# Relative bias table of a two-layer encoder: one copy in DRAM, read back with a positive step on SyncE's queue

## The chip, the cores and the metric

The kernel runs on one core of one Trainium2 chip. A time is the device time of one execution in microseconds (us); the kernel before takes 1199.93 us, the median of three runs (1199.75 to 1200.17). Engines are named as in the profile: PE is TensorE, DVE is VectorE, ACT is ScalarE, POOL is GpSimd, SP is SyncE. SP computes nothing here and only issues DMAs, which it does in the order of its program; SPq and ACTq in a row are the instructions by which SP and ACT issue DMAs.

## The reference

Two layers of an encoder over 256 tokens of width 1024, all float32:

```python
for i in range(DEPTH):                                       # DEPTH = 2
    h = x + 0.5 * swiglu(rms_norm(x, norm_ffn1[i]), w_ffn1_in[i], w_ffn1_out[i])   # D_FF = 2816
    u = rms_norm(h, norm_mix[i])
    q, k, v, c, g = split(u @ w_in[i])
    q, k = rms_norm per head (q_norm, k_norm)                # 8 query heads, 2 key heads of 64
    y_attn = window_attention(q, k, v, sink[i], rel_bias) @ w_attn_out[i]
    y_conv = silu(layer_norm(depthwise_conv(...))) @ w_conv_out[i]
    h = h + (sigmoid(g_attn) * y_attn + sigmoid(g_conv) * y_conv) @ w_o[i]
    h = h + 0.5 * swiglu(rms_norm(h, norm_ffn2[i]), w_ffn2_in[i], w_ffn2_out[i])
    x = h + (p[i] @ w_pe_proj[i]) * sigmoid(rms_norm(h, norm_pe[i]) @ w_pe_gate[i])
```

What the change is about lies in `window_attention`. The scores of a query at place q (0 to 127) of its block against a window of 384 keys get a bias that depends on the distance alone:

```python
rel = kj[None, :] - BLOCK - qi[:, None]          # qi: 0..127, kj: 0..383
bias = rel_bias[t5_buckets(rel)]                 # one value for each distance and head
s = where(valid, s + bias, NEG_INF)              # valid: |rel| <= 128 and inside the sequence
```

So the bias of one head is a table of 512 distances, and row q of the 128 x 384 matrix is that table shifted by one place for each q. The table and the matrix are the same in both layers.

## The kernel before

**Activations** lie with features on partitions, as blocks of 128 features by 256 tokens. Matrix products are made exact to float32 by splitting both operands into two float32r parts (hi and lo) and adding three products: lines 311, 312 and 313 in `mm3`.

**The weight stream** (class `Weights`) sets the pace of the work. SP loads raw weights in units of up to 1,024 KB into four buffers (line 76). From each unit, ACT casts a piece of 128 columns to its hi part (line 100) and DVE subtracts to get the lo part (line 101); such a piece is a spec. With every spec that PE takes (`get`), ACT and DVE are told to prepare the spec six further on (`LOOK`), and SP to load the unit two beyond its unit. Seven specs (`W_BUFS`) have room for their two parts. A raw buffer is free again when the casts and subtractions of its unit are done; then SP may issue the load of the unit four further on, and not before, and whatever DMA stands behind that load in SP's program waits with it.

**A feed-forward stage** (`ffn`) has 22 steps `gate_up(j)`, each two specs of 24 matmuls into one PSUM tile `ps_gu`, and then 8 steps `down(f)` into `ps_fo`. The evacuation of a step runs on DVE and ACT while PE does the next step. `hooks` is a table from j to a function that is called ahead of step j. In the first feed-forward stage of layer 0 it builds what later stages need: `late_loads` ahead of step 1 (small parameter loads, on SP's queue), `late_params` ahead of step 5, and `late_tables` ahead of step 6.

**The bias** is made in `late_tables`: a one-hot matrix of 33 x 512 picks the table of 8 heads x 512 distances with one product (`ps_rb`, line 522), DVE copies it to `tb` on 8 partitions (line 524), and then ACT issues two DMAs. The first (line 526) writes the table 128 times, once for each query, to the DRAM tile `tb_d` (128 x 8 x 512). The second (line 530) reads it back into `bias`, 128 partitions x 8 heads x 384, with a step that is one element short of a copy's length from partition to partition, so that partition q starts at place 127 - q. It reads what the first has written, so ACT waits for the first to land before it issues the second.

**The order** of the instructions on each engine comes from a scheduler that plays the program through with costs; it may move an instruction ahead of others by its priority. DMAs that are marked `keep_in_program_order` stay where the program puts them.

**The attention** runs inside the mixer (`mix`). `queries` transposes the normed queries into PSUM (`ps_qt`), and ACT copies them to `qT` (line 730), heads by tokens. `scores` multiplies a block of 128 queries with the keys (`ps_s`, line 745), so that queries lie on the partitions, and DVE adds the slice of `bias` (line 755). `gather` makes the output for the block (`ps_o`, line 792), with the queries along the free axis, and ACT copies it to `o` (line 799), which the products with `w_attn_out` (`ps_ao`, line 837) read later.

Of the kernel before, what the change touches and what calls it, by code (L numbers as in the profile page):

```python
# [15 lines left out]
P = 128  # L16
# [25 lines left out]
class Weights:  # L42
    """Streams the weights: DMA of raw float32 blocks, and their exact split into two
    float32r parts, in the order in which the tensor engine takes them. A spec without
    parts hands the raw block itself to the tensor engine."""

# [12 lines left out]
    def spec(self, k, n, pieces):  # L59
        """pieces: (unit, first k of the unit, first column of the unit, first column here, columns)."""  # L60
        self.specs.append((k, n, pieces, False))
# [53 lines left out]
    def later(self, n, fn):  # L115
        """Runs fn in front of the n-th get from here."""
        self.hooks.append((self.next_get + n - 1, fn))
# [21 lines left out]
def encoder_kernel(ctx: ExitStack, tc: tile.TileContext, a: dict, out: bass.AP):  # L139
# [17 lines left out]

    # ---------------------------------------------------------------- inputs
    ident = const.tile([P, P], F32, name="ident")
# [36 lines left out]

    # --------------------------------------------------------- weight stream
    ws = Weights(tc, raw_pool, w_pool)
# [90 lines left out]

    # ------------------------------------------------------------- constants  # L290
    ones_d = const.tile([P, P], F32, name="ones_d")
# [11 lines left out]

    # -------------------------------------------------------------- helpers
    def mm3(ps, w, x, first=True, last=True, k0=0, x_k0=0, n_k=None, cols=slice(0, P)):
# [9 lines left out]
    def pair(name, x, fresh):  # L315
        """Two products with x in one PSUM tile [P, 2, T]; right behind the evacuation that
        made x (fresh) its last block comes last."""
        if not fresh:
            ps = mm_tile(name).rearrange("p (c t) -> p c t", c=2)
            return ps, [lambda c=c: mm3(ps[:, c, :], ws.get(), x) for c in range(2)]  # L320
        ps = at_tile(name).rearrange("p (c t) -> p c t", c=2)[:, :, :T]
        w = []

        def start(c):
            w.append(ws.get())
            mm3(ps[:, c, :], w[c], x, last=False, n_k=KD - 1)

        def end():
            start(1)
            for c in range(2):  # L330
                mm3(ps[:, c, :], w[c], x, first=False, k0=KD - 1, x_k0=KD - 1, n_k=1)

        return ps, [lambda: start(0), end]
# [15 lines left out]
    def flush_urgent():  # L349
        """The last evacuation of a phase, which the next one waits for."""  # L350
        with tc.high_priority(offset=300):
            flush()

    def group(products, evac):
        """The products of one PSUM bank; its evacuation follows the first product of the next group."""
        for i, fn in enumerate(products):
            fn()
            if i == 0:
                flush()
        pending.append(evac)  # L360
# [8 lines left out]
    def newton(r, v, n):  # L369
        """r <- r * (1.5 - 0.5 * v * r * r)"""  # L370
        t = tmp.tile([P, n], F32, name="nwt", tag=f"nwt{n}")
        nc.gpsimd.tensor_tensor(out=t, in0=r, in1=r, op=ALU.mult)
        nc.gpsimd.tensor_tensor(out=t, in0=t, in1=v, op=ALU.mult)
        nc.gpsimd.tensor_scalar(out=t, in0=t, scalar1=-0.5, scalar2=1.5, op0=ALU.mult, op1=ALU.add)
        nc.gpsimd.tensor_tensor(out=r, in0=r, in1=t, op=ALU.mult)

    def table(func):
        """Loads a table of the scalar engine ahead of its use."""
        tc.keep_in_program_order(nc.scalar.preload_act_table(func))

    class gate:
        """Evacuations wait for the norm of the phase that they belong to."""

        ready = True

    class Stat:
        """The reciprocal root mean square r of x over its features, on every partition;
        with tokens on partitions as r_tok, and what it makes of eps behind it as eps_tok."""

# [39 lines left out]
    def emit_x(k, gain, xn, stat):  # L429
        """The next layer's operand x * gain of feature block k, split, and its squares."""  # L430
        src = x32[:, k, :]
        nc.scalar.activation(out=xn[0][:, k, :], in_=src, func=AF.Copy, scale=gain)
        nc.vector.scalar_tensor_tensor(
            out=xn[1][:, k, :], in0=src, scalar=gain, in1=xn[0][:, k, :].bitcast(F32),
            op0=ALU.mult, op1=ALU.subtract,
        )
        stat.add(src)
# [8 lines left out]

    # -------------------------------------------------------------- startup
    x_cur = new_x("xa", "x0")
# [28 lines left out]

    # tables for later phases, built while the first phase runs
    late = {}
# [25 lines left out]
    def late_tables(hp):  # L505
# [18 lines left out]
        nc.vector.tensor_copy(tb, ps[:NH, :NREL])  # L524
        tb_d = dram.tile([P, NH, NREL], F32, name="tb_d")
        nc.scalar.dma_start(tb_d.rearrange("q h m -> h q m"), tb.unsqueeze(1).broadcast_to([NH, P, NREL]))
        bias = const.tile([P, NH, 3 * P], F32, name="bias")
        base = tb_d[:, :, :]
        skew = bass.AP(base.tensor, base.offset + P - 1, [[NH * NREL - 1, P], [NREL, NH], [1, 3 * P]])
        nc.scalar.dma_start(bias, skew)  # L530
        late["bias"] = bias

    # ------------------------------------------------------------------ FFN
    def ffn(hp, l, x_in, stat_in, gain_name, xn, stat, hooks):
# [45 lines left out]

    # ---------------------------------------------------------------- mixer
    def mix(l, u, st, xn, stat):
        cw, kg, bias, sink = (late[n] for n in ("cw", "kg", "bias", "sink"))
        with tc.tile_pool(name="mix_pool", bufs=1) as mp:
# [18 lines left out]

            # ------------------------------------------------ gated conv input
            def conv_in(i):
# [20 lines left out]

            # ------------------------------------------- keys and values by token
            vt = mp.tile([P, 2, P], F32, name="vt")
# [3 lines left out]
            def head_norms(ps, heads):  # L632
                """1 / rms of each head, by token; eps stands behind the norm of x that ps has not seen."""
                n = 2 * heads
# [58 lines left out]

            # ------------------------------------------------- queries by token
            qn = mp.tile([P, 2, GROUP, 2, HD], F32, name="qn", tag="sqq")
            qT = mp.tile([P, GROUP, T], F32, name="qT")

            def queries():
# [23 lines left out]
                def turn():  # L722
                    pt = at_tile("ps_qt").rearrange("p (c t) -> p c t", c=GROUP)
                    for c in range(GROUP):
                        for t in range(2):
                            nc.tensor.transpose(
                                pt[:, c, t * P : (t + 1) * P], qn[:, t, c].rearrange("p v d -> p (v d)"), ident
                            )
                    for c in range(0, GROUP, 2):
                        nc.scalar.copy(out=qT[:, c : c + 2, :], in_=pt[:, c : c + 2, :])  # L730

# [3 lines left out]

            # -------------------------------------------------------- attention
            o = mp.tile([P, GROUP, T], F32, name="o")
# [49 lines left out]
            def gather(qb, v):  # L787
# [9 lines left out]
                if v == 1:  # L797
                    ov = o_ps.pop(qb).rearrange("p (c q) -> p c q", c=GROUP)
                    nc.scalar.copy(out=o[:, :, qb * P : (qb + 1) * P], in_=ov)

            # ------------------------------------------------------------ gates
            for at, fn in (
# [28 lines left out]

            # ----------------------------------------------------- branch outputs
            def products(ps, x):
# [75 lines left out]
            def mix_out(f, n):  # L909
                """Blocks f .. f + n; behind conv_out the first blocks take its last part at the end."""  # L910
                ps = at_tile("ps_wo").rearrange("p (c t) -> p c t", c=2)[:, :, :T] if n == 2 else None
# [31 lines left out]

    # --------------------------------------------------- per-layer embedding
    def embed(l, x_in, st, xn, stat):
# [64 lines left out]
    for l in range(L):  # L1010
        with tc.tile_pool(name="ffn1_pool", bufs=1) as hp:
            hooks = {1: lambda: late_loads(hp), 5: late_params, 6: lambda: late_tables(hp)} if l == 0 else {}
            xn, stat = new_x("xa", f"xm{l}"), Stat()
            ffn(hp, l, x_cur, st, "norm_mix", xn, stat, hooks)
# [14 lines left out]
def rel_onehot():  # L1029
    """One row for each bucket of the relative position j - 255, and one for positions beyond the window."""  # L1030
    import numpy as np
# [34 lines left out]
```

## Time and profile before

| | |
|---|---|
| runs | 1199.93 us median of 3 (1199.75 to 1200.17) |
| profiled execution | span 1195.8 us from its first to its last instruction; the profile shows no other time of it. The runs' median is 4.1 us above that span |
| PE busy | 1160.1 us, 97% of the span |
| DVE, ACT, POOL busy | 812.5 us, 613.9 us, 89.4 us |
| DMA | 205.07 MB, 171 GB/s on average |

How to read the rows: a row of the timeline or of the chain of waits begins with start and duration in us from the start of the span. A row of waits gives who waited for whom, the time in total, how often, and the longest one. In a row of windows the two ends and the length of the stretch come first, then each engine's busy time with the instructions (x), the granted PE clock (1.00 is full speed), the busy share of the DMA engines and GB/s.

### The profile page before, as it was taken

The numbers are of one execution on the slowest core, as the hardware profiler recorded it, in microseconds if no ns is written. First come the engines' busy times: TensorE is split into PE (matmuls) and PEld (weight loads), VectorE is DVE, ScalarE is ACT, GpSimd is POOL, SyncE is SP. The second block draws the span as 40 slices with busy tenths as digits, with TensorE's granted clock in tenths as the row PEclk, the third lists the DMA queues.
The fourth block names the chain that finished last, engine by engine and source line by source line (L and its number), as shares of the span: only waits on it lengthen the run. The fifth ranks groups of instructions, "written<-read, shape, count | busy, mean of one in ns | idle before, by whom it ended". The sixth has DMA issues, their size and how long they took to land.

```text
span 1195.8 us, 21809 instructions
## 1 busy us (share of the span) xinstructions
PE 1160.1 (97%) x9082; PEld 1125.0 (94%) x9082; DVE 812.5 (68%) x1214; ACT 613.9 (51%) x1033; POOL 89.4 (7%) x119
## 2 busy tenths in 40 slices
PE   7985999999999999999999999999999999999998
PEld 7985999999789999999999999999978899999997
DVE  5825765699767766665786666568986786666564
ACT  6614444477535544444674444447753564444443
POOL 3000001130001000000010000112100020000110
PEclk9996999999999999999999999999999999999999
DMA  8957645656136664555656555565531665644541
GB/s 248 288 99 209 229 151 173 215 179 152 59 105 205 193 211 158 188 180 175 200 162 210 169 179 163 194 212 177 142 106 36 213 220 175 199 154 159 194 142 36
DMA packets 196710, 205.07 MB, mean 171 GB/s; under 512 B 3731, under 2 KB 188899, under 8 KB 196612
## 3 DMA queue, kind: packets, MB, share of 16 engines
q1 hardware_dynamic: 194508, 200.01, 52.4%
q10 hardware_dynamic: 2104, 3.68, 1.9%
q8 instruction: 71, 1.16, 0.4%
q14 instruction: 27, 0.22, 0.1%
HBM read 200.53 MB, written 3.15 MB: 170 GB/s over the span
## 4 chain that ended last, share of the span: by engine, by line
PE 91%; DMA 5%; DVE 2%; ACT 1%; issue 0%; ACTq 0%
PE ps_gu L313 13%; PE ps_gu L311 13%; PE ps_gu L312 13%; PE ps_fo L312 7%; PE ps_fo L313 7%; PE ps_fo L311 7%; DMA tb_d<-tb 4%; PE ps_g L311 3%; PE ps_g L313 3%; PE ps_g L312 3%; PE ps_co L837 2%; PE ps_s L745 1%; PE ps_c L311 1%; PE ps_pe L313 1%; PE ps_pe L311 1%; PE ps_pe L312 1%
## 5 line engine op out<-in xcount | busy, mean ns | idle before, releaser
L101 DVE TENSOR_TENSOR w_lo<-raw,w_hi 128x1024 fp32r<-128x1024 f32 (+1 forms) x368 | 440.9, 1202 | 266.8 <-ACT w_hi L100 264.3
L100 ACT CAST w_hi<-raw 128x1024 fp32r<-128x1024 f32 (+1 forms) x368 | 377.4, 1030 | 443.2 <-PE ps_gu L312 196.7
L312 PE MATMUL ps_fo<-h_lo,w_hi 128*128 128x256 f32 x704 | 198.9, 283 | 0.0
L313 PE MATMUL ps_fo<-h_hi,w_lo 128*128 128x256 f32 x704 | 198.9, 283 | 0.0
L311 PE MATMUL ps_fo<-h_hi,w_hi 128*128 128x256 f32 x704 | 198.9, 283 | 0.0
L312 PEld LDWEIGHTS ps_fo<-h_lo,w_hi 128*128 128x128 f32 x704 | 135.1, 192 | 0.0
L311 PEld LDWEIGHTS ps_fo<-h_hi,w_hi 128*128 128x128 f32 x704 | 135.1, 192 | 0.0
L313 PEld LDWEIGHTS ps_fo<-h_hi,w_lo 128*128 128x128 f32 x704 | 135.1, 192 | 0.0
L400 POOL TENSOR_TENSOR sq_acc<-sq_acc,sq 128x256 f32<-128x256 f32 x56 | 56.3, 1005 | 924.7 <-ACT sq L399 924.2
L311 PE MATMUL ps_gu<-x0h,w_hi 128*128 128x256 f32 x352 | 102.6, 291 | 19.6 <-ACT w_hi L100 17.4
L313 PE MATMUL ps_gu<-x0h,w_lo 128*128 128x256 f32 x352 | 102.2, 290 | 0.7 <-DVE w_lo L101 0.7
L312 PE MATMUL ps_gu<-x0l,w_hi 128*128 128x256 f32 x352 | 101.8, 289 | 0.0
L600 DVE SCALAR_TENSOR_TENSOR y<-cpad,cw,y 128x256 f32<-128x256 f32 x240 | 101.1, 476 | 0.1
L312 PE MATMUL ps_gu<-xf1l,w_hi 128*128 128x256 f32 x352 | 100.0, 284 | 0.0
L311 PE MATMUL ps_gu<-xn0h,w_hi 128*128 128x256 f32 x352 | 100.0, 284 | 0.0
L312 PE MATMUL ps_gu<-xf0l,w_hi 128*128 128x256 f32 x352 | 99.9, 284 | 0.0
L311 PE MATMUL ps_gu<-xf1h,w_hi 128*128 128x256 f32 x352 | 99.9, 284 | 0.0
L311 PE MATMUL ps_gu<-xf0h,w_hi 128*128 128x256 f32 x352 | 99.8, 284 | 0.0
L313 PE MATMUL ps_gu<-xn0h,w_lo 128*128 128x256 f32 x352 | 99.8, 284 | 0.0
L313 PE MATMUL ps_gu<-xf1h,w_lo 128*128 128x256 f32 x352 | 99.8, 283 | 0.0
L313 PE MATMUL ps_gu<-xf0h,w_lo 128*128 128x256 f32 x352 | 99.8, 283 | 0.0
L312 PE MATMUL ps_gu<-xn0l,w_hi 128*128 128x256 f32 x352 | 99.8, 283 | 0.0
(222 smaller groups left out, 2727.9 us busy)
## 6 DMA issues: line engine op xcount, KB each, us to landing
raw<-in_w_ffn_in_dram SPq DMA_DIRECT2D x86, 1024.0 KB
raw<-in_w_in_dram SPq DMA_DIRECT2D x30, 1024.0 KB
raw<-in_w_ffn_out_dram SPq DMA_DIRECT2D x32, 896.0 KB
raw<-in_w_ffn_out_dram SPq DMA_DIRECT2D x16, 1024.0 KB
raw<-in_w_o_dram SPq DMA_DIRECT2D x8, 1024.0 KB
raw<-in_w_pe_gate_dram SPq DMA_DIRECT2D x8, 1024.0 KB
raw<-in_w_attn_out_dram SPq DMA_DIRECT2D x8, 512.0 KB
raw<-in_w_conv_out_dram SPq DMA_DIRECT2D x4, 1024.0 KB
```

The costliest lines, as they stand in the source:

```text
L100: nc.scalar.copy(out=hv[:, :, d0 : d0 + w], in_=src),
L101: nc.vector.tensor_tensor(out=lv[:, :, d0 : d0 + w], in0=src, in1=hv[:, :, d0 : d0 + w].bitcast(F32), op=ALU.subtract,),
L311: nc.tensor.matmul(ps, wh[:, k0 + k, cols], xh[:, kx, :], start=f, stop=False)
L312: nc.tensor.matmul(ps, wh[:, k0 + k, cols], xl[:, kx, :], start=False, stop=False)
L313: nc.tensor.matmul(ps, wl[:, k0 + k, cols], xh[:, kx, :], start=False, stop=e)
L400: nc.gpsimd.tensor_tensor(out=self.acc, in0=self.acc, in1=sq, op=ALU.add)
L600: nc.vector.scalar_tensor_tensor(out=y[:, i, :], in0=src, scalar=w, in1=y[:, i, :], op0=ALU.mult, op1=ALU.add)
L745: nc.tensor.matmul(ps[:, c, :], qT[v * HD : (v + 1) * HD, c, qb * P : (qb + 1) * P], kT[v * HD : (v + 1) * HD, :], start=True, stop=True,)
L837: nc.tensor.matmul(ps[:, c * T : (c + 1) * T], w[:, k, c * P : (c + 1) * P], x[:, k, :], start=k == 0, stop=k == KC - 1,)
```

## The change

The table is written to DRAM once (8 x 512) instead of 128 times. The read-back then steps by +1 element from partition to partition: partition r starts at place r of each head's table. So partition r holds the row of query 127 - r, and the queries of a block are laid down in reverse to match: ACT's copy to `qT` reads each block of 128 tokens from PSUM backwards, and ACT's copy to `o` reads them backwards again, which restores the order. Keys, values and everything behind `o` are unchanged.

Both DMAs go from ACT's queue to SP's, as functions of their own that are marked to stay in program order: `late_write` ahead of step 8 of the first feed-forward stage and `late_bias` ahead of step 12. Comments and docstrings that the change also deletes are left out of this diff.

```diff
         tb = hp.tile([NH, NREL], F32, name="tb")
         nc.vector.tensor_copy(tb, ps[:NH, :NREL])
-        tb_d = dram.tile([P, NH, NREL], F32, name="tb_d")
-        nc.scalar.dma_start(tb_d.rearrange("q h m -> h q m"), tb.unsqueeze(1).broadcast_to([NH, P, NREL]))
+        late["tb"] = tb
+
+    def late_write():
+        tb_d = dram.tile([NH, NREL], F32, name="tb_d")
+        tc.keep_in_program_order(nc.sync.dma_start(tb_d, late.pop("tb")))
+        late["tb_d"] = tb_d
+
+    def late_bias():
         bias = const.tile([P, NH, 3 * P], F32, name="bias")
-        base = tb_d[:, :, :]
-        skew = bass.AP(base.tensor, base.offset + P - 1, [[NH * NREL - 1, P], [NREL, NH], [1, 3 * P]])
-        nc.scalar.dma_start(bias, skew)
+        base = late.pop("tb_d")[:, :]
+        skew = bass.AP(base.tensor, base.offset, [[1, P], [NREL, NH], [1, 3 * P]])
+        tc.keep_in_program_order(nc.sync.dma_start(bias, skew))
         late["bias"] = bias
...
                     for c in range(0, GROUP, 2):
-                        nc.scalar.copy(out=qT[:, c : c + 2, :], in_=pt[:, c : c + 2, :])
+                        nc.scalar.copy(
+                            out=qT[:, c : c + 2, :].rearrange("p c (t q) -> p (c t) q", q=P),
+                            in_=pt[:, c : c + 2, :].rearrange("p c (t q) -> p (c t) q", q=P)[:, :, ::-1],
+                        )
...
-                    nc.scalar.copy(out=o[:, :, qb * P : (qb + 1) * P], in_=ov)
+                    nc.scalar.copy(out=o[:, :, qb * P : (qb + 1) * P], in_=ov[:, :, ::-1])
...
-            hooks = {1: lambda: late_loads(hp), 5: late_params, 6: lambda: late_tables(hp)} if l == 0 else {}
+            hooks = {1: lambda: late_loads(hp), 5: late_params, 6: lambda: late_tables(hp), 8: late_write, 12: late_bias} if l == 0 else {}
```

How the instructions move: on PE, DVE and POOL the order is the same, row for row. On ACT the two DMAs drop out and nothing else changes its place. ACT in the first feed-forward stage of layer 0, before, from the write of the table to just behind the read-back (L100 is the cast of a weight spec, L549 and L444 belong to evacuations):

```order
L526 DMA tb_d<-tb 8x128x512
L100 CAST w_hi<-raw 128x1024
L549 ACTIVATE sg<-gu 128x256
L100 CAST w_hi<-raw 128x1024
L444 CAST h_hi<-hh 128x256
L100 CAST w_hi<-raw 128x1024
L549 ACTIVATE sg<-gu 128x256
L100 CAST w_hi<-raw 128x1024
L444 CAST h_hi<-hh 128x256
L530 DMA bias<-tb_d 128x8x384
L100 CAST w_hi<-raw 128x1024
```

In the changed kernel the same nine casts and evacuations follow each other with neither DMA among them. SP in the same stage, now (L485 are the small loads of `late_loads`, L76 the weights):

```order
L485 DMA sink<-in_sink_dram 128x16
L76 DMA raw<-in_w_ffn_in_dram 128x8x256 x8
L529 DMA tb_d<-tb 8x512
L76 DMA raw<-in_w_ffn_in_dram 128x8x256 x4
L537 DMA bias<-tb_d 128x8x384
L76 DMA raw<-in_w_ffn_in_dram 128x8x256 x4
L76 DMA raw<-in_w_ffn_out_dram 128x8x256
```

Before, these 16 weight loads stood in one run behind the loads of `late_loads`. Now the write stands behind the 8th and the read-back behind the 12th of them; 4 loads of this stage's first weights and all of its second weights stand behind the read-back.

## Prediction

> **What bounds the kernel now.** I read the summary first, then PE's waits, then the chain of waits, and then PE's timeline around the place that the chain names. PE is the bound nearly everywhere:
>
> ```profile
> span 1195.8 us, 21809 instructions
> PE 1160.1 (97%) x9082; PEld 1125.0 (94%) x9082; DVE 812.5 (68%) x1214; ACT 613.9 (51%) x1033; POOL 89.4 (7%) x119
> ```
>
> So what a change elsewhere is worth is the PE idle time that it removes. The waits of PE, and those of ACT in the first 120 us, have one large entry each:
>
> ```profile
> PE ps_gu L311 <- ACT w_hi L100: 17.4, 1, 17.4
> ACT w_hi L100 <- DMA tb_d<-tb: 35.2, 1, 35.2
> ```
>
> PE waited once, 17.4 us, for a weight cast, and ACT waited once, 35.2 us, for the table's write. The chain of waits puts them in one line of cause:
>
> ```profile
> 55.20 0.60 DVE tb L524
> 55.82 44.68 DMA tb_d<-tb
> 100.52 0.40 ACTq L530
> 101.01 1.05 ACT w_hi L100
> 102.09 1.24 DVE w_lo L101
> 103.37 0.58 PE ps_gu L313
> 170.72 0.24 PE ps_fo L311 x2
> ```
>
> The write takes 44.68 us. ACT issues the read-back (line 530) only when it has landed, and ACT works in order, so the casts behind line 530 stand still until 101. PE lives on weights already prepared and then runs dry; ACT's 35.2 us less PE's 17.4 us says that this store lasts 17.8 us. Behind 103.37 the chain is PE's own work again.
>
> **What the stall costs.** PE's timeline at both ends of it:
>
> ```profile
> 84.44 0.28 PE L313 MATMUL ps_gu<-x0h,w_lo 128*128 128x256 f32 x1
> 102.11 0.58 PE L311 MATMUL ps_gu<-x0h,w_hi 128*128 128x256 f32 x1 [17.39 <-ACT w_hi L100]
> 108.02 0.41 PE L313 MATMUL ps_gu<-x0h,w_lo 128*128 128x256 f32 x1
> 108.41 0.28 PE L312 MATMUL ps_gu<-x0l,w_hi 128*128 128x256 f32 x1
> 108.53 0.28 PE L313 MATMUL ps_gu<-x0h,w_lo 128*128 128x256 f32 x1
> ```
>
> At full pace matmuls start 0.12 us apart (108.41, 108.53). The next one after 84.44 was due at 84.56 and came at 102.11: 17.55 us lost. From 102.11 on the matmuls are longer, 0.41 us instead of 0.28, until 108.41. Twenty-five of them start in these 6.30 us; at full pace they take 25 x 0.12 = 3.00, so 3.30 us more are lost. These rows show both ends of the slow stretch. Stall and slow restart together: 17.55 + 3.30 = **20.85 us**.
>
> A second way to the same number is to set this stage beside the same stage of layer 1, which has no tables to build; both windows run from one statistics product to the next:
>
> ```profile
> 25.24:231.68 206.44, 188.59 (x1540) 187.05 (x1539) 120.22 (x153) 90.66 (x132) 7.25 (x9) 0.95 0.65 194
> 617.70:807.60 189.90, 189.90 (x1582) 189.85 (x1582) 122.82 (x152) 91.70 (x131) 7.24 (x9) 1.00 0.58 189
> L510 PE MATMUL ps_cw<-ident,cw_ld x2: 268/269/270, 48.6 to 48.8; 124*128 124x124 f32 x2
> L522 PE MATMUL ps_rb<-onehot,rb x2: 589/590/592, 52.4 to 52.9; 33*8 33x512 f32 x2
> ```
>
> In layer 0 the first product comes two specs later in the stage (the code says behind 4 specs, against 2), so 48 matmuls, 5.76 us, must come off layer 1's 189.90; its own extra products (lines 510 and 522) add up to 2 x 0.27 + 2 x 0.59 = 1.7 us, less where they overlap. Without a stall the window should take about 185.9 us, and it takes 206.44: 20.6 us. The two ways agree within 0.3 us, so nothing else of note is lost in this stage.
>
> **The change, part by part.** *The wait on ACT.* Line 530 leaves ACT, and no other instruction of ACT waits for the table before the attention. The casts then go on as they do in layer 1. The gain is the 20.85 us. What would be late next is PE itself: in layer 1, at the same work, ACT waits for PE at every cast.
>
> *The write.* It shrinks from 2048.0 KB to 16 KB and is issued by SP when `tb` is there:
>
> ```profile
> tb_d<-tb ACTq DMA_DIRECT2D x1, 2048.0 KB
> bias<-tb_d ACTq DMA_DIRECT2D x1, 1536.0 KB
> 52.25 3.35 SPq L76 DMA_DIRECT2D raw<-in_w_ffn_in_dram  x2
> 63.93 0.37 SPq L76 DMA_DIRECT2D raw<-in_w_ffn_in_dram  x1
> 1190.24 1.80 DMA out_dram<-ot
> ```
>
> The 7th and 8th of the 16 loads are the pair that ends at 55.60, and the copy to `tb` ends at 55.8. So SP waits 0.2 us for `tb` in a gap that lasts until 63.93 in any case: nothing. The landing of this write is bounded below by a store of the output, 1.80 us, and above by the old write, 44.68 us; I take the lower one, as 16 KB is nearer to the output's 128 KB than to 2048 KB.
>
> *The read-back* is as large as before but stands in SP's program, with weights behind it. SP's rhythm in layer 1, where nothing disturbs it, with the DMA share and ACT's casts of that time:
>
> ```profile
> 683.73 0.37 SPq L76 DMA_DIRECT2D raw<-in_w_ffn_in_dram  x1
> 686.61 0.37 SPq L76 DMA_DIRECT2D raw<-in_w_ffn_in_dram  x1
> 695.25 3.25 SPq L76 DMA_DIRECT2D raw<-in_w_ffn_in_dram  x2
> 675.80:687.30 11.50, 11.50 (x98) 11.50 (x97) 7.61 (x11) 5.42 (x9) 0.00 (x0) 1.00 0.57 183
> 681.39 1.05 ACT L100 CAST w_hi<-raw 128x1024 fp32r<-128x1024 f32 x1 [1.53 <-PE ps_gu L312]
> 684.27 1.05 ACT L100 CAST w_hi<-raw 128x1024 fp32r<-128x1024 f32 x1 [1.51 <-PE ps_gu L312]
> 101.70:107.10 5.40, 0.50 0.96 330
> ```
>
> Two loads 2.9 us apart, then 8.6 us of nothing, every 11.5 us. The read-back is the instruction right behind the second load of a pair (the 12th), so it falls into such a gap, about 23 us behind the write (two pairs), near 79 us. A write that lands within 23 us is not waited for. The read is 1,536 KB, 1.57 MB; just after the old issue the DMA engines moved 330 GB/s at a share of 0.96, and at that rate it takes 4.8 us (an estimate, as the row does not say whose bytes these are). The DMA engines are idle 43% of each 11.5 us, 4.9 us. It fits. If it does not, there are reserves. A load is issued six casts before its first cast is due, 6 x 2.88 = 17.3 us, and needs 1.05 MB / 330 GB/s = 3.2 us. ACT feels the read only when it takes more than 8.6 + 17.3 - 3.2 = 22.7 us, and PE only 17.8 us later, at 40.5 us. The bounds of its price are 4.8 us (the old rate) and 34 us (the rate of the old write, 2.10 MB in 44.68 us or 47 GB/s); PE pays nothing at either. Were the cover gone, it would pay the 4.8 us. Should the write take 44.68 us again, SP would be held some 22 us longer, and 22 + 4.8 is still below 40.5: nothing.
>
> The Trainium skill, page "DMA: Bandwidth & Descriptors", section "Queues, rings and completion order", speaks against this part: each DMA engine takes turns between the issuers' queue rows, but within one row it consumes descriptors in order. By that rule the read could share with the weights on ACT's row, and on SP's row the weights behind it wait for all of it. By the rule alone the sum would be 4.8 us worse; by the 0.57 share it is nothing, and I go by the share.
>
> *The backward copies.* ACT's copies keep their sizes and only read PSUM in the other direction, which no row of this trace shows.
>
> ```profile
> 273.54 1.20 ACT L730 COPY qT<-ps_qt 128x512 f32<-128x512 f32 x2
> 276.00 1.99 PE L745 MATMUL ps_s<-kT,qT 64*128 64x256 f32 x8
> L716 ACT ACTIVATE qn<-ps_q,rh 128x64 f32<-128x64 f32 x32 | 6.8, 365 | 5.6 <-POOL rh L375 5.6
> 329.04 0.59 ACT L799 COPY o<-ps_o 128x512 f32<-128x512 f32 x1 [0.78 <-PE ps_o L792]
> 334.78 1.03 PE L837 MATMUL ps_ao<-o,raw 128*128 128x256 f32 x4
> ```
>
> The pair to `qT` ends at 274.74 and the scores start at 276.00, 1.26 us of slack; the later copy to `o` ends at 329.63 and is first read at 334.78, 5.15 us of slack. Bounds: nothing (the same number of elements), or four times the time: the dearest element that ACT reads from PSUM in this trace is that of the short line 716, 365 ns / 64 = 5.7 ns, against 715 ns / 512 = 1.4 ns for line 730 now. Then the pair takes 4.8 us instead of 1.2, 2.3 us beyond the slack, in each of two layers: 4.6 us. Twice the time stays within the slack. A gain is excluded, since the copies are not on PE's path. I take nothing: the nearest row to the backward copy is the forward one, with the same elements from the same banks; line 716 is dear because it is short.
>
> **Sum.** On the profiled execution 1195.8 - 20.85 = 1174.95 us. With the 4.1 us between span and median kept: 1199.93 - 20.85 = **1179.1 us**.
>
> **The rivals.** *The backward read is slow* (four times): 1179.1 + 4.6 = 1183.7 us. For it speaks only that the trace has no such access; 6%.
>
> *The weights wait behind the read-back* in SP's row, and the reserve is not there when it is needed, because this stage fills its buffers while it starts: 1179.1 + 4.8 = 1183.9 us. Against it is ACT's row right behind the old write, where it waits for PE and not for data; 6%.
>
> ```profile
> 56.45 1.05 ACT L100 CAST w_hi<-raw 128x1024 fp32r<-128x1024 f32 x1 [2.50 <-PE ps_gu L313]
> ```
>
> *The read-back is very slow*, the one that ends on the other side. All 128 partitions now read the same 16 KB of DRAM, where they read 2 MB before. If such reads serve each other badly, SP's row is held and PE runs dry from 40.5 us on; from 40.5 + 20.85 = 61 us, 26 GB/s, the kernel is slower than before. At 16 GB/s the read takes 98 us and the kernel 1179.1 + 98 - 40.5 = 1237 us. For it: the trace has no read like it. Against: it needs 13 times less than 330 GB/s. Slower than before 2%; between 40.5 and 61 us, a part of the gain lost, 2%.
>
> *The change does not do what it says*: PE's stall came from raw weights that arrived late, and the write only coincided. Then 1199.9 us. Against: when ACT came free at 101.01 the raw block was there, and the chain holds nothing but the write; 3%.
>
> **How the numbers follow.** My forecast holds 81%, the five others 6, 6, 2, 2 and 3%. Range 1178.0 to 1183.0 us: 1.1 us below for the 0.3 us between the two ways of counting and the runs' own spread, and above up to just short of the two cases near 1184, of which smaller forms fall inside. It leaves about 18% out. A measurement of this kernel can tell about 0.2% (2.4 us) from no change. Faster by more than that: 81 + 6 + 6 + 2 = 95%; the same 3%; slower 2%.
>
> **What the profile of the changed kernel would show.** PE's wait for `w_hi` of 17.4 us is gone, no 35.2 us wait on ACT, and the granted clock stays at 1.00 from the start-up to the end. The window between the statistics products of layer 0's first stage is near 185.6 us (206.44 - 20.85). SP issues the write near 56 us and the read-back near 79 us, and its weight loads behind that keep the 11.5 us rhythm, with no wait of ACT for raw weights. Lines 730 and 799, under their new numbers, keep 0.72 and 0.59 us. Wrong would be: a wait of PE for `w_hi` near 90 to 130 us (the read-back), a wait of PE at `ps_s` (the copies), or a first stage as long as before.

## The result, and the profile after

The changed kernel takes 1176.97 us (median of 4 runs, 1176.52 to 1177.24); before, measured beside it, takes 1200.05 us (4 runs, 1199.75 to 1201.21). The ratio is 0.9816, 95% interval 0.9804 to 0.9828: 23.1 us less. The forecast was 1179.1 us with a range from 1178.0. So the direction and the mechanism came out, and the time lies 2.1 us below the forecast and 1.0 us below the range.

The profiled execution has the span that the sum gave, 1174.7 us where 1174.95 was worked out. The summary, and PE's largest waits, which held the 17.4 us before:

```profile
span 1174.7 us, 21809 instructions
PE 1156.8 (98%) x9082; PEld 1121.5 (95%) x9082; DVE 813.6 (69%) x1214; ACT 614.2 (52%) x1033; POOL 88.5 (8%) x119
PE ps_par L190 <- DMA rows_first<-in_norm_ffn_dram: 3.3, 1, 3.3
PE ps_var L876 <- ACT ysq L871: 3.2, 2, 1.6
```

ACT's waits between the write and the end of the stage (57 to 210 us) are nearly all for PE, as in layer 1, and none is for raw weights or for the table:

```profile
ACT w_hi L100 <- PE ps_gu L312: 41.8, 27, 1.9
ACT w_hi L100 <- PE ps_fo L312: 32.8, 23, 1.8
ACT h_hi L444 <- DVE hh L558: 2.2, 2, 1.1
ACT sg L556 <- DVE gu L552: 1.5, 1, 1.5
ACT w_hi L100 <- issue: 1.1, 1, 1.1
```

The two ends of the first feed-forward stage are the statistics products, of before and then of the changed kernel, from the chain of waits:

```profile
25.24 0.43 PE ps_stat L409 x2
231.68 0.43 PE ps_stat L409 x2
```

```profile
24.47 0.43 PE ps_stat L409 x2
210.44 0.43 PE ps_stat L409 x2
```

The stage takes 210.44 - 24.47 = 185.97 us instead of 206.44: 20.5 us less, where 20.85 was forecast. Behind it nothing moved: 964.1 us were left before (1195.8 - 231.68), and 964.3 are left now. The start is 0.8 us shorter in this execution. So the spans differ by 21.1 us, and the runs by 23.1.

SP's queue around the two DMAs, the DMA engines just behind the read-back, and ACT's casts at that time:

```profile
57.29 0.30 SPq L529 DMA_DIRECT2D tb_d<-tb  x1
63.53 0.37 SPq L76 DMA_DIRECT2D raw<-in_w_ffn_in_dram  x1
77.93 0.37 SPq L76 DMA_DIRECT2D raw<-in_w_ffn_in_dram  x1
78.35 0.57 SPq L537 DMA_DIRECT2D bias<-tb_d  x1
86.58 3.25 SPq L76 DMA_DIRECT2D raw<-in_w_ffn_in_dram  x2
78.40:86.60 8.20, 1.00 1.06 362
84.24 1.05 ACT L100 CAST w_hi<-raw 128x1024 fp32r<-128x1024 f32 x1 [1.53 <-PE ps_gu L312]
87.12 1.05 ACT L100 CAST w_hi<-raw 128x1024 fp32r<-128x1024 f32 x1 [1.52 <-PE ps_gu L312]
```

The read-back is issued at 78.35 (79 was forecast), right behind a weight load, and SP issues the next one at 86.58, as it would anyway. The DMA engines are full in the gap, 362 GB/s, and ACT goes on at 2.88 us a cast, waiting for PE alone. By the trace's record of landings, the load just ahead of the read-back landed at 83.19, the read-back at 88.77, and the load that SP issued behind it at 86.58 landed at 91.71, 5.1 us after its issue. The load issued at 683.73 in layer 1 of the kernel before, which nothing disturbs, takes as long (it landed at 688.83).

### The profile page after: what moved, and what is told of

It reads as the page before. It is cut to its first block, busy times and chain, and to the rows that moved or that the text cites. A ratio compares the mean times of both kernels' runs of the same rounds, so it can differ in the third digit from the quotient of the medians.

```text
span 1174.7 us, 21809 instructions
## 1 busy us (share of the span) xinstructions
PE 1156.8 (98%) x9082; PEld 1121.5 (95%) x9082; DVE 813.6 (69%) x1214; ACT 614.2 (52%) x1033; POOL 88.5 (8%) x119
## 4 chain that ended last, share of the span: by engine, by line
PE 96%; DVE 2%; DMA 1%; ACT 1%; issue 0%; SPq 0%; ACTq 0%
PE ps_gu L313 14%; PE ps_gu L311 14%; PE ps_gu L312 14%; PE ps_fo L313 7%; PE ps_fo L312 7%; PE ps_fo L311 7%; PE ps_g L311 3%; PE ps_g L313 3%; PE ps_g L312 3%; PE ps_co L847 2%; PE ps_s L755 1%; PE ps_c L311 1%; PE ps_pe L313 1%; PE ps_pe L312 1%; PE ps_pe L311 1%; PE ps_c L313 1%
## 5 line engine op out<-in xcount | busy, mean ns | idle before, releaser
L100 ACT CAST w_hi<-raw 128x1024 fp32r<-128x1024 f32 (+1 forms) x368 | 377.2, 1030 | 427.0 <-PE ps_gu L312 215.3
```

What stands on the lines that cost most here:

```text
L100: nc.scalar.copy(out=hv[:, :, d0 : d0 + w], in_=src),
```

## The experiments

Four questions: which of the edits carries the gain, whether 17.8 us of prepared weights is what decides, whether the backward copies cost anything, and why the time came out 2.1 us lower than the sum. Each kernel was timed beside runs of the kernel before on its own chip.

### The size of the write alone

The changed kernel, with both DMAs put back on ACT's queue. The scheduler does not put the read-back quite where it stood: four of ACT's instructions lie between the two DMAs, where eight lay before.

```diff
-        late["tb"] = tb
+        tb_d = dram.tile([NH, NREL], F32, name="tb_d")
+        nc.scalar.dma_start(tb_d, tb)
+        bias = const.tile([P, NH, 3 * P], F32, name="bias")
+        base = tb_d[:, :]
+        skew = bass.AP(base.tensor, base.offset, [[1, P], [NREL, NH], [1, 3 * P]])
+        nc.scalar.dma_start(bias, skew)
+        late["bias"] = bias
...
-            hooks = {..., 6: lambda: late_tables(hp), 8: late_write, 12: late_bias} if l == 0 else {}
+            hooks = {..., 6: lambda: late_tables(hp)} if l == 0 else {}
```

> The changed kernel with both DMAs back on ACT's queue where they stood before; only the size of the write, the positive step and the backward copies are kept. Theory (the wait on ACT is as long as the write, and a write of 16 KB lands in 2 to 5 us): ACT waits at the read-back for less than 3 us, PE not at all, 1177.0 us within 0.5 us of the changed kernel. Rival (the queue matters by itself: ACT must not wait for a DMA, or the read beside the weights costs them their rate): 1180 us or more, with a wait of PE for w_hi.

Measured: 1177.23 us (4 runs), ratio to before 0.982 (0.9806 to 0.9835), within 0.3 us of the changed kernel. ACT's timeline there:

```profile
55.65 0.51 ACTq L526 DMA_DIRECT2D tb_d<-tb  x1
60.03 0.40 ACT L444 CAST h_hi<-hh 128x256 fp32r<-128x256 f32 x1
60.30 0.40 ACTq L530 DMA_DIRECT2D bias<-tb_d  x1
61.95 1.05 ACT L100 CAST w_hi<-raw 128x1024 fp32r<-128x1024 f32 x1 [1.53 <-PE ps_gu L312]
```

The read-back follows the write by 4.65 us, and the cast behind it waits for PE, not for the table. Shrinking the write carries the whole gain; once the write is short, leaving ACT's queue adds nothing to it.

### The queue alone

The kernel before, with its 2048 KB write and its old read-back moved to SP's queue at the places of the changed kernel, and forward copies:

```diff
-        nc.scalar.dma_start(tb_d.rearrange("q h m -> h q m"), tb.unsqueeze(1).broadcast_to([NH, P, NREL]))
+        tc.keep_in_program_order(
+            nc.sync.dma_start(tb_d.rearrange("q h m -> h q m"), tb.unsqueeze(1).broadcast_to([NH, P, NREL]))
+        )
...
-        nc.scalar.dma_start(bias, skew)
+        tc.keep_in_program_order(nc.sync.dma_start(bias, skew))
...
+    hooks = {..., 6: lambda: late_tables(hp), 8: late_write, 12: late_bias}
```

> The kernel before with its large write and its old read-back both on SP's queue, at the places of the changed kernel, and no backward copies. Theory A (weights behind the write in SP's row wait for it on the DMA engines that it uses): the write is issued near 57 us and ends near 99 us; the weight load issued at 63.5 us is due at 80.8 us, and PE runs dry 17.8 us later, near 98.6 us, so PE idles 3 to 8 us and restarts slowly: 1180 to 1188 us. Theory B (only SP's wait for the landing counts, as the prediction had it, 26.6 us against a reserve of 40.5 us): no wait of PE, 1177.0 us.

Measured: 1189.43 us (4 runs, 1187.18 to 1189.55), ratio 0.9915 (0.9898 to 0.9931). About 12 us above the changed kernel. From the chain of waits, the waits of ACT and of PE:

```profile
63.99 40.45 DMA raw<-in_w_ffn_in_dram
ACT w_hi L100 <- DMA raw<-in_w_ffn_in_dram: 42.3, 9, 27.1
PE ps_gu L311 <- ACT w_hi L100: 9.3, 1, 9.3
```

A weight load issued at 63.99 landed 40.45 us later, at 104.4. The write, issued ahead of it on the same queue at 57.0, landed at 101.4. ACT waited 27.1 us for the load, PE 9.3 us; with 3.2 us for the slow restart that makes the 12.5 us over the changed kernel. Theory B, by which only SP's own wait for the landing counts, falls: it gave 1177.0. Theory A has the wait for the write and misses the size by 1.4 us at its upper end; it reckoned that the write would end at 99. The prediction had put this case at nothing. The store of prepared weights is the same as before, 27.1 - 9.3 = 17.8 us.

That the two share a queue is only a small part of it. In the kernel before, with the write on ACT's queue, SP issued loads at 63.93 and 66.81, and by the trace's record of landings they landed at 100.71 and 103.39, after 36.8 and 36.6 us. A load lands in 16 parts, as many as there are DMA engines, and this write in 8. Eight parts of each of the two loads landed within 7.1 us. The other eight came as late as the write, which landed at 100.50, or later: from 100.28 on for the first load, from 102.94 on for the second. A window of the kernel before in that time:

```profile
85.00:101.00 16.00, 0.00 (x0) 0.00 (x0) 0.00 (x0) 0.00 (x0) 0.00 (x0) 0.59 0.51 80
```

The DMA engines are half busy (share 0.51) and move 80 GB/s. By these numbers the write occupies half of the engines, and the parts of a load that need this half come late from either queue. The shared queue adds some 3.7 us (40.45 against 36.8). In the kernel before this lay hidden behind ACT's own wait. The present kernel shows what is left when ACT no longer waits: 8.4 us of the gain are there (1197.87 - 1189.43), and the rest needs the short write.

### More copies on ACT's queue

The kernel of the first experiment with 64 and with 96 copies written and the first one read:

```diff
-        tb_d = dram.tile([NH, NREL], F32, name="tb_d")
-        nc.scalar.dma_start(tb_d, tb)
+        tb_d = dram.tile([64, NH, NREL], F32, name="tb_d")
+        nc.scalar.dma_start(tb_d.rearrange("q h m -> h q m"), tb.unsqueeze(1).broadcast_to([NH, 64, NREL]))
```

> The kernel of e2_write_only (both DMAs on ACT's queue, backward copies), but the table is written 64 times instead of once; the read-back uses the first copy. Theory (ACT is held until the write lands, and PE lives on 17.8 us of prepared weights): the write takes 4.3 + 64/128 x 40.4 = 24.5 us, lands near 80.3 us, ACT idles 14.5 us, less than 17.8 us, so PE does not wait at all: 1177.2 us within 0.7 us. Rival (the loss grows with the length of the write, about half of it for half the copies): near 1187 us.

> The same with 96 copies. Theory: the write takes 4.3 + 96/128 x 40.4 = 34.6 us and lands near 90.4 us, ACT idles 24.8 us, PE 24.8 - 17.8 = 7.0 us, and the clock is halved at the restart, 1.7 to 3.4 us more: 1186 to 1188 us, and its runs scatter more widely than those of the changed kernel, by up to the 1.7 us of the restart. Rival (proportional loss): near 1192 us.

Measured: 64 copies 1176.97 us (2 runs; ratio 0.982, 0.9801 to 0.984), 96 copies 1191.48 us (4 runs, 1190.7 to 1192.52; ratio 0.9939, 0.9923 to 0.9956). With 64 copies, ACT is held and PE never notices:

```profile
78.52 0.40 ACTq L530 DMA_DIRECT2D bias<-tb_d  x1
79.02 0.42 ACT L548 ACTIVATE sg<-gu 128x256 f32<-128x256 f32 x1 [17.18 <-DMA tb_d<-tb]
```

With 96 copies, ACT's wait and PE's:

```profile
ACT h_hi L444 <- DMA tb_d<-tb: 29.0, 1, 29.0
PE ps_gu L311 <- ACT w_hi L100: 12.1, 1, 12.1
```

One copy 1177.2, 64 copies 1177.0, 96 copies 1191.5, 128 copies about 1198: a loss in proportion falls with the 64 copies, which cost nothing though ACT idles 17.2 us. I had expected 14.5 us; the read-back stands three instructions earlier in ACT's order than in the kernel before, so nearly the whole store was used up. With 96 copies the size that I expected was wrong by 3.5 us. This kernel issues the write at 57.8 instead of 55.8, and its read-back stands a cast and an evacuation earlier in ACT's order than in the kernel before, so ACT is held from 63.6 to 92.6 us, 29.0 us instead of 24.8, with 16.9 us of weights in store. PE's 12.1 us and a slow restart of 3.5 us make 15.6 us, as much as the profiled execution, the longest of the four, lies above the changed kernel (1192.52 - 1176.97). The narrow scatter expected of the changed kernel, and a wider one here, both came: 0.7 us against 1.8 us.

### No reversal

```diff
-                        nc.scalar.copy(
-                            out=qT[:, c : c + 2, :].rearrange("p c (t q) -> p (c t) q", q=P),
-                            in_=pt[:, c : c + 2, :].rearrange("p c (t q) -> p (c t) q", q=P)[:, :, ::-1],
-                        )
+                        nc.scalar.copy(out=qT[:, c : c + 2, :], in_=pt[:, c : c + 2, :])
...
-                    nc.scalar.copy(out=o[:, :, qb * P : (qb + 1) * P], in_=ov[:, :, ::-1])
+                    nc.scalar.copy(out=o[:, :, qb * P : (qb + 1) * P], in_=ov)
```

> The changed kernel without the reversal: the copies to qT and o read forward as before, so each query gets the bias row of another query of its block. Theory (the direction of the copies costs nothing): 1177.0 us within 0.5 us. Rival (the backward read is part of why the time came out 2.1 us below the forecast, by another pace of ACT in the attention): 1178.5 us or more.

Measured: 1177.43 us (4 runs, 1177.26 to 1177.83), ratio 0.9821 (0.9807 to 0.9836), within 0.5 us of the changed kernel. In the changed kernel the copies themselves, with the backward read:

```profile
L737 ACT COPY qT<-ps_qt x4: 586/654/720, 252.3 to 828.4; 128x512 f32<-128x512 f32 x4
L809 ACT COPY o<-ps_o x4: 586/587/589, 287.6 to 883.9; 128x512 f32<-128x512 f32 x4
```

They take 586 to 720 ns and 586 to 589 ns. Read forward, the copies to `qT` take 586 to 594 ns in this run and 708 to 721 ns in the kernel before, so their time varies for another reason; those to `o` take 585 to 589 ns in both. The direction costs nothing.

### Where the other two microseconds are

> The kernel before, unchanged, to see how its spans stand to its times. Theory A (the profiled execution shown of before was shorter than its usual ones, and the time outside the span is the same 1.8 us as in the changed kernel): the spans of these runs are near 1198.2 us, 1.8 us below their times, and the profile shows 23 us lost at the stall (idle and slow restart) instead of 20.85. Theory B (about 4.1 us lie outside the span of the kernel before, 2.3 us more than in the changed one): spans near 1195.8 us at times near 1199.9 us, and the stall at 20.85 us again.

> The kernel before once more, for the parts in which one execution of it differs from another. The run is 1.8 us above its span. Theory C (the slow restart behind the stall is what varies): the stall is 17.4 us again, the stretch of half clock behind it is between 3.4 and 6.9 us long, and a longer span goes with a longer stretch. Theory D (the write's length varies): the stall itself differs by as much as the span does. Theory E (the start varies, as it does in the changed kernel): the first statistics product, at 24.1 to 25.7 us so far, comes later by as much as the span is longer.

> The same once more, for a further execution: theories C, D and E as for e7_before_look2.

> The kernel before, a further execution. From the looks so far: its span less the first statistics product (25.1, 24.1, 25.3, 25.6 us) is 1170.6 to 1171.5 us and follows ACT's wait for the write (35.2, 35.2, 35.5, 36.0 us). If the write's length and the start are all that varies, span = start + 1135.4 us + ACT's wait, within 0.3 us, here too, and a time near 1200 us has a wait of 37 us or more. If something else makes the slow executions, a span of 1198 us comes with a wait of at most 36 us and an early start.

> The same, for a further execution, with the same two theories as e9_before_look4.

> The same, for a further execution, with the same two theories as e9_before_look4.

> The changed kernel, unchanged, beside many runs of the kernel before on one chip, to see which gain is the usual one. Theory A (the gain is the stall and the slow restart, 20.85 us in the profile shown of before, up to 1.5 us more in executions with a longer wait for the write; the 23.1 us of the first comparison hold a long set of runs of before): median of before 1197.5 to 1198.5 us, the changed kernel 1176.8 to 1177.5 us, a gain of 20.3 to 21.5 us. Theory B (23 us is the gain): the changed kernel comes out 22.5 us or more below before here too.

Every run lies 1.7 to 1.9 us above its own span, of the kernel before as of the changed one: the profiled run of the changed kernel 1176.52 against 1174.7, of e1_before_again 1196.46 against 1194.7. So theory A of e1 is right in its first half. An execution with a span of 1195.8 us takes 1197.6, not 1199.9. The 4.1 us that the prediction took to lie outside the span were 1.8 us outside it, and 2.3 us by which the profiled execution was shorter than the three runs shown. Its second half, a stall that costs 23 us, was not seen in e1: there the stall is as it was, and the span is shorter still.

The kernel before scatters: 10 runs of e1 and 13 beside them go from 1195.9 to 1200.0. What varies, in seven profiled executions of it (start is the first statistics product; the slow stretch goes from PE's restart to its first matmul at full pace):

| execution | span | start | ACT's wait for the write | PE's wait for w_hi | slow stretch |
|---|---|---|---|---|---|
| shown before | 1195.8 | 25.1 | 35.2 | 17.4 | 6.3 |
| e1 | 1194.7 | 24.1 | 35.2 | 17.5 | 5.7 |
| e7 | 1196.4 | 25.3 | 35.5 | 17.7 | 6.1 |
| e8 | 1197.1 | 25.6 | 36.0 | 18.2 | 5.7 |
| e9 | 1197.1 | 25.0 | 37.2 | 19.4 | 3.9 |
| e10 | 1197.2 | 26.0 | 35.4 | 17.6 | 6.8 |
| e11 | 1195.7 | 25.0 | 35.5 | 17.7 | 5.4 |

The rule written down for e9 to e11, span = start + 1135.4 + ACT's wait within 0.3 us, gives 1197.6, 1196.8 and 1195.9; it holds for e11 and misses e9 by -0.5 and e10 by +0.4. The slow stretch is the rest: at half pace, half of it is lost. The span less start, PE's wait and half of the slow stretch is 1150.1 to 1150.8 us in all seven, while the spans lie 2.5 us apart. In the changed kernel, which has no stall, the span less its start is 1174.7 - 24.3 = 1150.4 us, and in e2 and e4 it is 1149.8 and 1149.9. So within a microsecond PE's wait and the slow restart are all that the change takes away, 20.3 to 21.4 us in these seven. PE's timeline of e9, and then of e10:

```profile
104.25 0.58 PE L311 MATMUL ps_gu<-x0h,w_hi 128*128 128x256 f32 x1 [19.44 <-ACT w_hi L100]
108.02 0.31 PE L312 MATMUL ps_gu<-x0l,w_hi 128*128 128x256 f32 x1
108.17 0.28 PE L313 MATMUL ps_gu<-x0h,w_lo 128*128 128x256 f32 x1
```

```profile
103.28 0.58 PE L311 MATMUL ps_gu<-x0h,w_hi 128*128 128x256 f32 x1 [17.61 <-ACT w_hi L100]
109.83 0.37 PE L313 MATMUL ps_gu<-x0h,w_lo 128*128 128x256 f32 x1
110.04 0.28 PE L311 MATMUL ps_gu<-x0h,w_hi 128*128 128x256 f32 x1
```

The long wait of e9 is followed by a short slow stretch, and the other way round in e10. So theories C, D and E each hold a part: the restart, the write's length and the start all vary. Only the start varies in the changed kernel too (24.3 to 25.7 us over its profiled executions and those of e2, e4 and e5).

The last run gives the gain once more: changed 1177.18 us (5 runs), before 1198.45 us (9 runs, 1197.1 to 1200.68), ratio 0.9819 (0.9806 to 0.9833): 21.3 us, inside theory A's 20.3 to 21.5. For e2 the gain to before's median of 1197.87 is 20.6 us, for e5 (median of before 1197.77) 20.8 us. The first comparison, 23.1 us, has the longest set of runs of before. No profiled execution is as long as 1200 us. The three parts can add up to it: the largest start, wait and slow stretch seen lie 0.9, 2.0 and 0.5 us above those of the execution shown before. That they did so in each of those four runs is not shown. Of the 45 other runs of the kernel before only 5 reach the shortest of the four, 1199.75 us, so four in a row are hardly chance; what those four had in common stays open.

## Why the prediction was right or wrong

**The stall and its cost** (17.55 + 3.30 = 20.85 us): right. The stage got 20.5 us shorter, and the later runs give a gain of 21.3 us for the changed kernel and of 20.6 and 20.8 us for e2 and e5. That the span came out 0.25 us from the sum is partly luck, as the profiled execution also started 0.8 us earlier.

**The step that failed** is the last of the sum: "With the 4.1 us between span and median kept". The 4.1 us were not a constant around the span. 1.8 us of them are, and with 1174.95 + 1.8 the forecast would have been 1176.75, where 1176.97 was measured. The other 2.3 us belonged to the runs of before: their stall and start differ from one execution to the next, and the execution shown had the shortest wait of PE of the seven. The part of that scatter that sits in the stall goes with the change; how the 2.3 us were divided in those runs is not shown, but the runs of the changed kernel have only 0.2 us of them. I subtracted the stall of a short execution from the median of long ones. The range, 1.1 us downward, had the same fault: it held the counting error of the stall (0.3 us) and the spread of the three runs (0.4 us), and nothing for the gap between those runs and the profile, which stood in plain sight as 4.1 us.

**The write**: right in that SP waits 0.2 us for `tb` and that nothing stands behind it in that gap; it was issued 1.3 us later than reckoned. It landed at 62.01, 4.7 us after its issue, where the sum took 1.80 us from the output's store; the read-back is issued 21 us behind it, so nothing came of that.

**The read-back**: right that it costs nothing, at its place and with the DMA engines' spare time: the load behind it landed in 5.1 us. (At the rate of the old write the read would take 33.5 us, not 34.) The Trainium skill's rule on the order within a queue row ("DMA: Bandwidth & Descriptors", section "Queues, rings and completion order"), which I set aside for the spare share, agrees with e3, where weights behind 2048 KB on one row took 40.45 us to land. But e3 does not test it alone, since weights on the other row took 36.8 us beside the same write. The sum did not change because the read fits into the gap, not because the rule is weak.

**"Should the write take 44.68 us again ... nothing"**: wrong. It counted SP's wait for the landing and left out that the weights issued while the write is under way are late too. e3 measured 12 us for it. It had no part in the result, as the write is now short.

**The backward copies**: right, nothing; e4 and the copies' own durations show it.

**The rivals** (backward read slow, weights waiting behind the read-back, very slow read, no effect) all fell; the read from one 16 KB place moved at the full rate of the DMA engines. What was held against the second of them was read wrongly, though. At 56.45 the write had only just been issued, and ACT was casting weights that had landed earlier; the loads issued next took 36.8 us. The rival fell because the read is short, not because a long transfer leaves the weights alone.

## What to carry to other kernels

A DMA issue that waits for another DMA holds every instruction behind it on its engine. Its price is that wait less the work that the bounding engine has in store, plus a slow restart, and nothing below that: 17.2 us of wait were free here, 35.2 us cost 20.85. Shrink what is waited for first. Moving a long transfer to another queue frees the engine that waited, but not the loads that need the same DMA engines: here that brought 8.4 us of 20.6. When a profiled span is carried over to a median of runs, ask whether the gap between them is a constant of all kernels or scatter of this one: a stall that varies from run to run takes its scatter along when it goes.

## What was not expected of the hardware

The end of the half clock behind the stall does not follow PE's restart. In the trace's records of the granted clock it lasts 20.48 us in all seven executions of the kernel before, though PE's wait goes from 17.4 to 19.4 us, and 13.65 us in both kernels with a shorter stall (9.3 and 12.1 us). So a longer wait can get a shorter slow restart, 3.9 us after 19.4, against 6.8 after 17.6. The Trainium skill, page "TensorE: Matmul & The Clock Gate", Part 1, gives a free-running window of 3,413 ns; the two lengths are six and four of these.

A write of 2 MB from 8 partitions moved 47 GB/s and landed in 8 parts instead of 16. While it ran, 1 MB of weights took 36.8 us to land from another queue and 40.45 us from the same one, where a load in layer 1 took 5.1 us with nothing beside it.
